# The same hybrid block with its SBUF tile pools placed at other ends of the memory

## The chip, the cores and the metric

The kernel runs on one NeuronCore of a Trainium2 chip. The metric is the device time of one execution in microseconds, lower is better; a time that is given for a kernel is the median of several runs.

## What is computed

One layer of a hybrid decoder trunk on 512 tokens of 1024 features, in float32. Its matrix products are the bulk of it:

```python
h = _rmsnorm(x, g_mix)
proj = h @ w_in                       # 1024 -> 7424: LRU, gelu gate, q, k, v, memory q, 3 branch gates
y_lru = (gelu(gate_lru) * rg_lru(conv(x_lru))) @ w_lru_out
y_dil = dilated_attention(q, k, v, rel_bias) @ w_dil_out
y_mem = cross_attention(q_mem, _rmsnorm(mem, g_mem) @ w_mem_kv) @ w_mem_out
merged = gt[0] * y_lru + gt[1] * y_dil + gt[2] * y_mem
x = x + merged @ w_out
x = x + jnp.square(jax.nn.relu(_rmsnorm(x, g_mlp) @ w_mlp_in)) @ w_mlp_out
y = _rmsnorm(x, g_final)
```

## The kernel before, in words

**Precision and the three products.** Each float32 operand of a large product is split in two float32r parts: a high part (`whi`, `hT_hi`, `ah`, ...) that ScalarE makes by a copy, and a remainder (`wlo`, `hT_lo`, `al`, ...) that VectorE makes by a subtraction. A product is then three matmuls into one PSUM bank: high by high, high by low, low by high. Weights come as a raw slab by DMA from SyncE's queue (`raw`, two buffers), are split by `split_w` (line 162) into `whi` and `wlo` (four buffers each), and are used.

**Two kinds of product.** A matmul has a stationary operand (128 columns, brought in by a weight load, PEld in the profile) and a moving one (here mostly 512 columns).
- `mm3` (lines 186 to 195) makes features by tokens: the *weights* are stationary and the activations move. Per row block k it issues L191 (`whi` with the high activation), L192 (`whi` with the low one), L193 (`wlo` with the high one). The moving tiles are `hT_hi`, `hT_lo` (the normalised, transposed x), later `hmT_hi`, `hmT_lo` (the same for the MLP), and for the branch projections `y`, `odh`/`odl` and `omh`/`oml`.
- `out_step` (lines 932 to 938) makes tokens by features: the *activations* are stationary and the weights move. It issues L936 (high activation, `whi`), L937 (high activation, `wlo`), L938 (low activation, `whi`). It is used for the output projection, where the activations are the eight `mrg` tiles, and for the second MLP product. The trace names the weights before the activations there, as in `ps<-whi,act`.
- `v_proj` (L513 to L515) and the value half of the memory projection (L763 to L765) have the second form too, with `hT` and `mT` as the stationary side. `half_proj` (L247 to L251) has the first with 256 columns.

**The MLP.** It runs in four quarters of 1024 hidden features: `mlp_in(q + 1)` is issued ahead of `mlp_out(q)`. `mlp_evac` (line 973) writes the eight hidden chunks of a quarter: the first three into two tiles each of a ring called `q` (names `ah` and `al`), the other five into one pair tile each, `act`, which holds the high and the low part. `mlp_out` goes twice (two column halves) through k = 0 to 7 and within each k through the four token tiles: 36 matmuls of 512 columns that load `ah` or `al`, then 60 that load `act`. The last half of the last quarter goes token tile by token tile, and its last tile in two pieces of 256 columns.

**Order.** TensorE's order is the program's own, interleaved by a hand-written clock (`_Interleave`): attention and LRU steps are slipped between the dense groups. The other engines' instructions are placed by the tile framework.

**Where tiles lie.** A tile pool takes its place in each partition of SBUF when it is opened. Before, the pools stand one above the other in the order in which they are opened: `cst`, `big`, `wp` (raw and split weights), `sm` (small statistics), and on top of them the pool of the stage: `start`, then `lru`, then `att`, then `ep`. So the weights lie in the middle, `hT` and the rings `q`, `V` and `y4` below them, and the stage's own tiles above.

Of the kernel before, what the change touches and what calls it, by code (L numbers as in the profile page):

```python
# [17 lines left out]
P = 128  # L18
# [34 lines left out]
def _bucket_onehots():  # L53
    """[33, 3, 384]: column m of group g picks the bias row at its offset; row 32 marks masked offsets."""
    oh = np.zeros((NUM_BUCKETS + 1, 3, 384), np.float32)
    m = np.arange(384)
    for g in range(3):
        if g == 0:
            off = 255 - m
            valid = (off >= 0) & (off <= 128)  # L60
            dist = off
        elif g == 1:
            off = 127 - m
            valid = off >= 0
            dist = 4 * off
        else:
            off = 127 - m
            valid = (off >= 0) & (off % 4 == 0)
            dist = 4 * off
        b = _bucket(np.maximum(dist, 0))  # L70
        for j in m:
            oh[b[j] if valid[j] else NUM_BUCKETS, g, j] = 1.0
    return oh


def _head_select():
    """[4, 2, 128]: column p of pair hp picks head 2*hp + p // 64."""
    s = np.zeros((HPG, 2, P), np.float32)
    for hp in range(2):
        for p in range(P):  # L80
            s[2 * hp + p // HD, hp, p] = 1.0
    return s


class _Engine:
    """An engine whose instructions can be pinned to program order."""
# [16 lines left out]
class _Interleave:  # L103
    """Program order: dense matmul groups advance a clock; side generators yield the delay (in us of
    tensor-engine work) that their next step should stay behind."""
# [34 lines left out]
def hybrid_block(ctx: ExitStack, tc: tile.TileContext, x, mem, g_mix, w_in, b_gate, conv_w, conv_b,  # L140
# [7 lines left out]
    cst = ctx.enter_context(tc.tile_pool(name="cst", bufs=1))  # L148
    big = ctx.enter_context(tc.tile_pool(name="big", bufs=1))
    wp = ctx.enter_context(tc.tile_pool(name="wp", bufs=1))  # L150
    sm = ctx.enter_context(tc.tile_pool(name="sm", bufs=1))
# [24 lines left out]
    def slab(parts):  # L176
        """parts: (weight, first column) of 128 columns each; yields the split halves one by one."""
        raw = raw_tile(KT, 256)
        if parts[0][0] is parts[1][0] and parts[0][1] + P == parts[1][1]:
            nc.sync.dma_start(raw, cols(parts[0][0], parts[0][1], 256))  # L180
        else:
            for i, (w, c0) in enumerate(parts):
                nc.sync.dma_start(raw[:, :, i * P:(i + 1) * P], cols(w, c0, P))
        return [split_w(raw[:, :, i * P:(i + 1) * P], KT, P) for i in range(len(parts))]

    def mm3(ps, w, act, nk, k0=0, us=0.648):
        """ps = w.T @ act over nk row blocks, w = (hi, lo) stationary, act(k) -> (hi, lo) moving."""
        whi, wlo = w
        for k in range(nk):
            ah, al = act(k)  # L190
            PE.matmul(ps, whi[:, k0 + k, :], ah, start=k == 0, stop=False)  # L191
            PE.matmul(ps, whi[:, k0 + k, :], al, start=False, stop=False)  # L192
            PE.matmul(ps, wlo[:, k0 + k, :], ah, start=False, stop=k == nk - 1)  # L193
            if k % 2 == 1 and k < nk - 1:
                sch.tick(2 * us)
        # the caller ticks the rest after its evacuation

# [9 lines left out]
    def rstd(xt, sq, tag):  # L207
        """sq: scratch as wide as xt; returns [P, 1] rsqrt(mean(x^2) + eps)."""
        ss = sm.tile([P, 1], F32, name="ss", tag="ss" + tag, bufs=2)
        A.activation(sq, xt, AF.Square, accum_out=ss)  # L210
        return rstd_of(ss, tag)
# [12 lines left out]
    def transp(hn, dst, t):  # L224
        """hn [tokens, D] of token tile t, transposed and split into dst = (hi, lo)."""
        for half in range(2):
            ps = psum()
            for k in range(4):
                c = half * 4 + k
                PE.transpose(ps[:, k * P:(k + 1) * P], hn[:, c * P:(c + 1) * P], ident)  # L230
            pv = ps.rearrange("p (k n) -> p k n", k=4)
            hv = dst[0][:, half * 4:half * 4 + 4, t * P:(t + 1) * P]
            A.activation(hv, pv, AF.Copy)
            V.tensor_sub(dst[1][:, half * 4:half * 4 + 4, t * P:(t + 1) * P], pv, f(hv))
# [4 lines left out]
    def half_proj(items, act, evac, mid):  # L239
        """items: split stationaries; two token halves, the second after mid() was emitted."""  # L240
# [21 lines left out]
    T0 = big.tile([P, HPG, 256], F32, name="T0")  # L262
    T12 = big.tile([P, HPG, 2, P], F32, name="T12")
# [12 lines left out]
    # the tensor engine's clock gate opens while the first tokens are on their way  # L276
# [19 lines left out]
    # per-feature vectors, one column per 128 features  # L296
# [49 lines left out]
    def lru_gate(c, xc, xh, xlo, rg_hi, rg_lo):  # L346
# [12 lines left out]
        # t = tanh(-log(a) / 2) = (1 - a) / (1 + a); 1 / (1 + t) starts from (1 + a) / 2  # L359
# [22 lines left out]
    def start_rest():  # L382
        """the other two token tiles, the constants, then what the first LRU chunk needs."""
        for t in (2, 3):
            transp(hns[t], hT, t)

    def small_consts():
# [9 lines left out]
        # Toeplitz bias tiles: 128 copies of each vector, read back with a row pitch one short  # L397
# [16 lines left out]
    # softplus(-lam) = max(-lam, 0) + log1p(exp(-|lam|)), log1p(e) = 2 atanh(e / (2 + e))  # L414
# [52 lines left out]
    # block-diagonal recurrence gates, two 64-blocks per 128 features  # L467
# [14 lines left out]
    def qk_proj(g, nm):  # L482
        """two chunks (heads 0-1, 2-3) of q (scaled) or k; groups 1, 2 in residue order (t mod 4, t // 4)."""
        o = (O_Q if nm == "q" else O_K) + g * 256
        res = []
        for w in slab([(w_in, o), (w_in, o + P)]):
            ps = psum()
            mm3(ps, w, hmov, KT)
            t_ = q2k(nm)
            sc = 0.125 if nm == "q" else 1.0  # L490
            if g == 0:
                A.activation(t_, ps, AF.Copy, scale=sc)
            else:
                A.activation(t_.rearrange("p (r i) -> p r i", r=4), ps.rearrange("p (i r) -> p r i", r=4),
                             AF.Copy, scale=sc)
            res.append(t_)
            sch.tick(1.3)
        return res

    def v_proj(g):  # L500
        """[128 tokens, 4 token tiles, 256]; token tile = block for group 0, residue for groups 1, 2,
        which are brought to residue order on their way through DRAM."""
        vt = big.tile([P, 4, 256], F32, name="vt", tag="V", bufs=4)
# [18 lines left out]
        vr = big.tile([P, 4, 256], F32, name="vr", tag="V", bufs=4)  # L522
# [3 lines left out]
    def vtile(name):  # L526
        return big.tile([P, D], F32, name=name, tag="V", bufs=4)

    # memory tokens, normalised here and transposed once there is room
# [44 lines left out]
    def softmax_stats(sc, mz, i):  # L574
        """sc [P, 4 heads, n]: exp(s - max) in place; mz[:, 0|1, i, :] = max, sum."""
# [11 lines left out]
    def p_T(groups):  # L587
        """groups of 4 [128, 128] slices, transposed; returns SBUF tiles [128 keys, 4, 128 queries]."""
# [32 lines left out]
    def av_out(dst, view, terms):  # L621
        """terms: (transposed P [keys, 4, queries], V [keys, 256]) summed into [128, 2 head pairs, 128]."""
# [38 lines left out]
    def stats_T(mz, permute):  # L661
        """mz [P tokens, 2, 4 tiles, 4 heads] -> [4 heads, 2, 512 tokens] in token order."""
# [15 lines left out]
    def side_b():  # L678
# [13 lines left out]
        # merge by the softmax denominators  # L692
# [156 lines left out]
    def pair_m():  # L849
        return big.tile([P, 2, S], F32, name="m", tag="V", bufs=4)  # L850

    def pair_gate(c2, b):
        tg = big.tile([P, 2, S], F32, name="tg", tag="V", bufs=4)
# [56 lines left out]
    def act_tile(name):  # L910
        return ep.tile([P, 2, S], F32R, name=name, tag="act", bufs=10)
# [61 lines left out]
    def mlp_evac(act, ps):  # L973
        i = len(act)
        r = big.tile([P, 2, S], F32, name="rl", tag="V", bufs=4)
# [3 lines left out]
        else:  # L979
            t_ = act_tile("act")  # L980
# [96 lines left out]
```

## Time and profile before

| | us |
|---|---|
| median of three runs | 894.89 |
| lowest and highest run | 893.42 and 896.57 |
| span of the profiled execution, first to last instruction | 892.8 |
| TensorE busy in that span | 879.6 |
| VectorE, ScalarE, GpSimd busy | 451.6, 356.7, 26.0 |

The page gives no time of its own for the profiled execution; its span is 2.1 us under the median of the runs. TensorE's busy time is a union of matmuls that overlap in the pipeline: one matmul of 512 columns shows about 390 ns, yet the next one starts some 230 ns later. How fast TensorE goes is therefore read from the starts in the timeline (start to start), not from the durations. A duration still tells fast and slow matmuls apart, because it is longer by as much as the next start is later.

### The profile page before, as it was taken

How to read it: one execution, taken by the hardware profiler on the slowest of the kernel's cores; microseconds unless marked ns; L12 is line 12 of the kernel's file. 1: busy time of each engine (PE TensorE's matmuls, PEld its weight loads, DVE VectorE, ACT ScalarE, POOL GpSimd, SP SyncE). 2: the span in 40 equal slices, each digit the busy share in tenths (PEclk: the TensorE clock that was granted, in tenths of full speed). 3: DMA queues.
4: the chain of work that ended last, by engine and by line, in shares of the span. 5: the costliest groups of instructions: out<-in, count | busy, mean ns of one | idle time of the engine just before them, and what ended most of it. 6: DMA issues, size and time to landing. Idle time of an engine off the chain costs nothing.

```text
span 892.8 us, 10656 instructions
## 1 busy us (share of the span) xinstructions
PE 879.6 (99%) x4383; PEld 734.8 (82%) x4383; DVE 451.6 (51%) x628; ACT 356.7 (40%) x565; POOL 26.0 (3%) x34
## 2 busy tenths in 40 slices
PE   8999999999999999999999999999999999999997
PEld 7788888889888888888888888888888888888886
DVE  5778666764678543343424365444334433443342
ACT  5457666654644532332323154433113311441122
POOL 3110000000000000000000000000000000000020
PEclk9899999999999999999999999999999999999999
DMA  7673333333421222332434214322333323332202
GB/s 239 186 227 95 95 95 95 95 111 127 140 85 60 70 96 71 118 97 81 130 133 160 83 46 144 95 94 96 94 96 97 106 90 97 111 105 93 98 6 94
DMA packets 79164, 94.87 MB, mean 106 GB/s; under 512 B 3611, under 2 KB 64103, under 8 KB 78988
## 3 DMA queue, kind: packets, MB, share of 16 engines
q1 hardware_dynamic: 77916, 88.15, 31.6%
q0 software_dynamic: 1056, 5.52, 1.9%
q8 instruction: 34, 0.56, 0.3%
q10 hardware_dynamic: 144, 0.52, 0.1%
q14 instruction: 14, 0.11, 0.0%
HBM read 91.03 MB, written 5.52 MB: 108 GB/s over the span
## 4 chain that ended last, share of the span: by engine, by line
PE 92%; DVE 2%; DMA 2%; ACT 1%; issue 1%; POOL 0%; SPq 0%; POOLq 0%; ACTq 0%; DVEq 0%
PE ps L191 19%; PE ps L192 19%; PE ps L193 18%; PE ps L938 8%; PE ps L936 8%; PE ps L937 8%; PE ps L513 1%; PE ps L515 1%; PE ps L514 1%; DMA x<-in_x_dram 1%; PE ps L248 1%; PE ps L626 1%; PE ps L247 1%; PE ps L593 1%; PE ps L251 1%
## 5 line engine op out<-in xcount | busy, mean ns | idle before, releaser
L95 DVE TENSOR_TENSOR wlo<-raw,whi 128x1024 fp32r<-128x1024 f32 (+1 forms) x153 | 182.9, 1199 | 314.2 <-ACT whi L95 309.7
L95 ACT ACTIVATE whi<-raw 128x1024 fp32r<-128x1024 f32 (+1 forms) x154 | 159.5, 1037 | 394.2 <-PE ps L192 223.0
L191 PE MATMUL ps<-hT_hi,whi 128*128 128x512 f32 x400 | 156.6, 392 | 0.0
L193 PE MATMUL ps<-hT_hi,wlo 128*128 128x512 f32 x400 | 155.9, 390 | 0.0
L192 PE MATMUL ps<-hT_lo,whi 128*128 128x512 f32 x400 | 155.9, 390 | 0.0
L192 PE MATMUL ps<-hmT_lo,whi 128*128 128x512 f32 x240 | 93.4, 389 | 0.0
L193 PE MATMUL ps<-hmT_hi,wlo 128*128 128x512 f32 x240 | 93.4, 389 | 0.0
L191 PE MATMUL ps<-hmT_hi,whi 128*128 128x512 f32 x240 | 93.2, 389 | 0.0
L191 PEld LDWEIGHTS ps<-hT_hi,whi 128*128 128x128 f32 x400 | 75.1, 188 | 16.4 <-issue 0.6
L193 PEld LDWEIGHTS ps<-hT_hi,wlo 128*128 128x128 f32 x400 | 75.1, 188 | 15.8
L192 PEld LDWEIGHTS ps<-hT_lo,whi 128*128 128x128 f32 x400 | 75.1, 188 | 15.2
L938 PE MATMUL ps<-whi,act 128*128 128x512 f32 (+1 forms) x165 | 64.1, 389 | 0.0
L937 PE MATMUL ps<-wlo,act 128*128 128x512 f32 (+1 forms) x165 | 64.1, 388 | 0.0
L936 PE MATMUL ps<-whi,act 128*128 128x512 f32 (+1 forms) x165 | 64.1, 388 | 0.0
L192 PEld LDWEIGHTS ps<-hmT_lo,whi 128*128 128x128 f32 x240 | 45.1, 188 | 9.3
L191 PEld LDWEIGHTS ps<-hmT_hi,whi 128*128 128x128 f32 x240 | 45.0, 188 | 9.4
L193 PEld LDWEIGHTS ps<-hmT_hi,wlo 128*128 128x128 f32 x240 | 45.1, 188 | 9.3
L95 DVE TENSOR_TENSOR x<-x,ps 128x512 f32<-128x512 f32 (+1 forms) x41 | 27.7, 675 | 24.9 <-PE ps L938 24.6
L938 PE MATMUL ps<-whi,al 128*128 128x512 f32 (+1 forms) x99 | 38.0, 384 | 0.0
L937 PE MATMUL ps<-wlo,ah 128*128 128x512 f32 (+1 forms) x99 | 37.9, 383 | 0.0
L936 PE MATMUL ps<-whi,ah 128*128 128x512 f32 (+1 forms) x99 | 37.9, 383 | 0.0
L937 PEld LDWEIGHTS ps<-wlo,act 128*128 128x128 f32 x165 | 31.0, 188 | 7.1
(253 smaller groups left out, 1355.6 us busy)
## 6 DMA issues: line engine op xcount, KB each, us to landing
raw<-in_w_in_dram SPq DMA_DIRECT2D x23, 1024.0 KB
raw<-in_w_mlp_in_dram SPq DMA_DIRECT2D x16, 1024.0 KB
raw<-in_w_mlp_out_dram SPq DMA_DIRECT2D x16, 1024.0 KB
raw<-in_w_in_dram SPq DMA_DIRECT2D x12, 512.0 KB
raw<-in_w_mem_kv_dram SPq DMA_DIRECT2D x4, 1024.0 KB
raw<-in_w_out_dram SPq DMA_DIRECT2D x4, 1024.0 KB
x<-in_x_dram SPq DMA_DIRECT2D x7, 512.0 KB
raw<-in_w_lru_out_dram SPq DMA_DIRECT2D x4, 768.0 KB
```

The lines of the kernel that those rows point to most:

```text
L95: r = fn(*a, **k)
L191: PE.matmul(ps, whi[:, k0 + k, :], ah, start=k == 0, stop=False)
L192: PE.matmul(ps, whi[:, k0 + k, :], al, start=False, stop=False)
L193: PE.matmul(ps, wlo[:, k0 + k, :], ah, start=False, stop=k == nk - 1)
L247: PE.matmul(ps[:, sl], whi[:, k, :], ah, start=k == 0, stop=False)
L248: PE.matmul(ps[:, sl], whi[:, k, :], al, start=False, stop=False)
L251: PE.matmul(ps[:, sl], wlo[:, k, :], act[0][:, k, sl], start=False, stop=k == KT - 1)
L513: PE.matmul(ps[:, 0:256], ah, hi[:, k % 4, :], start=k == 0, stop=False)
L514: PE.matmul(ps[:, 0:256], ah, lo[:, k % 4, :], start=False, stop=False)
L936: PE.matmul(ps, ah[:, sl], hi[:, k % 2, :], start=k == 0, stop=False)
L937: PE.matmul(ps, ah[:, sl], lo[:, k % 2, :], start=False, stop=False)
L938: PE.matmul(ps, al[:, sl], hi[:, k % 2, :], start=False, stop=k == KT - 1)
```

## The change

Four edits, and comments and docstrings taken out (later lines stand three further down in the new kernel):

- `sm` and `wp` are opened with `side="right"`: they are allocated from the high end of SBUF downwards.
- A new pool `ot`, also from the high end, takes tiles that only VectorE, ScalarE and DMAs use, or that `v_proj` makes: `T0`, `T12` and the ring `V`, which were in `big`.
- The pair tiles `act` have a ring of eight instead of ten, and the fourth hidden chunk of each quarter goes into a ring of `big` (`y4`, six buffers, of which the residual tiles `x2` hold four), under the name `act3`.
- All else stays in `cst`, `big` and the stage pools, which are now allocated from the low end without the weights between them.

```diff
     cst = ctx.enter_context(tc.tile_pool(name="cst", bufs=1))
     big = ctx.enter_context(tc.tile_pool(name="big", bufs=1))
-    wp = ctx.enter_context(tc.tile_pool(name="wp", bufs=1))
-    sm = ctx.enter_context(tc.tile_pool(name="sm", bufs=1))
+    sm = ctx.enter_context(tc.tile_pool(name="sm", bufs=1, side="right"))
+    wp = ctx.enter_context(tc.tile_pool(name="wp", bufs=1, side="right"))
+    ot = ctx.enter_context(tc.tile_pool(name="ot", bufs=1, side="right"))
...
-    T0 = big.tile([P, HPG, 256], F32, name="T0")
-    T12 = big.tile([P, HPG, 2, P], F32, name="T12")
+    T0 = ot.tile([P, HPG, 256], F32, name="T0")
+    T12 = ot.tile([P, HPG, 2, P], F32, name="T12")
...
-        vt = big.tile([P, 4, 256], F32, name="vt", tag="V", bufs=4)
+        vt = ot.tile([P, 4, 256], F32, name="vt", tag="V", bufs=4)
...
-        return ep.tile([P, 2, S], F32R, name=name, tag="act", bufs=10)
+        return ep.tile([P, 2, S], F32R, name=name, tag="act", bufs=8)
...
-        r = big.tile([P, 2, S], F32, name="rl", tag="V", bufs=4)
+        r = ot.tile([P, 2, S], F32, name="rl", tag="V", bufs=4)
...
-            t_ = act_tile("act")
+            t_ = act_tile("act") if i > 3 else big.tile([P, 2, S], F32R, name="act3", tag="y4", bufs=6)
```

(The other tiles of the ring `V`, which are `vr`, `mn`, `msq`, `gbmem`, `m` and `tg`, go from `big` to `ot` in the same way.)

The built programs hold the same instructions in the same order on every engine. One wait is added: the DMA that loads `gbmlp` (SyncE's queue, line 237) also waits for the first software DMA, `bd<-bvec`. What changes is the addresses. In KiB from the start of a partition, as the two programs have them:

| tiles | used by TensorE as | before | after |
|---|---|---|---|
| `ident` | moving (transposes) | 16 | 16 |
| `hT_hi`, `hT_lo`, `hmT_hi`, `hmT_lo` | moving, in `v_proj` stationary | 18.3 to 50.3 | 18.3 to 50.3 |
| ring `q` (`q`, `k`, `ah`, `al`, `omh`, `odh`, ...) | moving or stationary | 74.3 to 98.3 | 50.3 to 74.3 |
| ring `y4` (`y`; after, `act3` too) | moving; `act3` stationary | 98.3 to 122.3 | 74.3 to 98.3 |
| `whi`, `wlo` | stationary in `mm3`, moving in `out_step` | 138.3 to 170.3 | 190.4 to 222.4 |
| `mT`, later `qmh`, `qml` | moving or stationary | 171.8 to 187.8 | 98.3 to 114.3 |
| `mrg`, `act` (ring of 10, then of 8) | stationary | 171.8 to 211.8 | 98.3 to 130.3 |
| `xh`, `xlo` / `rg_hi`, `rg_lo` | moving / stationary | 181.9 to 189.9 / 197.9 to 209.9 | 108.3 to 116.3 / 124.3 to 136.3 |
| `pr`, `prm` | stationary (transposes) | 187.8 to 199.8 | 114.3 to 126.3 |
| `pT`, `pTh`, `pTl` | moving | 199.8 to 207.8 | 126.3 to 134.3 |
| `km` / `vm` | moving / stationary | 207.8 to 215.8 / 215.8 to 223.8 | 134.3 to 142.3 / 142.3 to 150.3 |
| `vt`, `vr`, `mn` (ring `V`) | stationary | 58.3 to 74.3 | 158.4 to 174.4 |
| `raw` | not used | 122.3 to 138.3 | 174.4 to 190.4 |

## Rows read from the trace of the kernel before

**Rows 1.** The page: busy time by engine, TensorE's clock, the chain that ended last.
```profile
PE 879.6 (99%) x4383; PEld 734.8 (82%) x4383; DVE 451.6 (51%) x628; ACT 356.7 (40%) x565; POOL 26.0 (3%) x34
...
PEclk9899999999999999999999999999999999999999
...
PE 92%; DVE 2%; DMA 2%; ACT 1%; issue 1%; POOL 0%; SPq 0%; POOLq 0%; ACTq 0%; DVEq 0%
```

**Rows 2.** Matmuls grouped by line and shape: count | busy us, mean ns | idle.
```profile
L193 PE MATMUL ps<-hT_hi,wlo 128*128 128x512 f32 x400 | 155.9, 390 | 0.0
...
L192 PE MATMUL ps<-hmT_lo,whi 128*128 128x512 f32 x240 | 93.4, 389 | 0.0
...
L938 PE MATMUL ps<-whi,act 128*128 128x512 f32 x155 | 61.3, 396 | 0.0
...
L936 PE MATMUL ps<-whi,ah 128*128 128x512 f32 x93 | 36.2, 389 | 0.0
...
L938 PE MATMUL ps<-whi,mrg 128*128 128x512 f32 x64 | 25.3, 395 | 0.0
...
L192 PE MATMUL ps<-y,whi 128*128 128x512 f32 x48 | 18.7, 389 | 0.0
```

**Rows 3.** Timeline, TensorE, second MLP product: from `al` to `act`. Start us, duration us.
```profile
629.43 0.40 PE L938 MATMUL ps<-whi,al 128*128 128x512 f32 x1
629.67 0.39 PE L936 MATMUL ps<-whi,act 128*128 128x512 f32 x1
```

**Rows 4.** Timeline, TensorE: the last `act` of that half, then `ah` again.
```profile
643.43 0.40 PE L938 MATMUL ps<-whi,act 128*128 128x512 f32 x1
643.66 0.39 PE L936 MATMUL ps<-whi,ah 128*128 128x512 f32 x1
```

**Rows 5.** Timeline, TensorE: the first `act` of the next column half.
```profile
651.83 0.39 PE L936 MATMUL ps<-whi,act 128*128 128x512 f32 x1
```

**Rows 6.** Timeline, TensorE: the last `mm3` matmul before the output projection.
```profile
484.74 0.40 PE L193 MATMUL ps<-omh,wlo 128*128 128x512 f32 x1
```

**Rows 7.** Matmuls grouped by line and shape: smaller groups with both operands above 138 KiB.
```profile
L191 PE MATMUL ps<-mT_hi,whi 128*128 128x256 f32 x32 | 9.4, 295 | 0.0
...
L764 PE MATMUL ps<-wlo,mT_hi 128*128 128x512 f32 x16 | 6.3, 395 | 0.0
...
L351 PE MATMUL ps<-xlo,rg_hi 128*128 128x512 f32 x12 | 4.7, 395 | 0.0
...
L797 PE MATMUL ps<-km,qmh 128*128 128x256 f32 x16 | 4.5, 281 | 0.0
```

**Rows 8.** Timeline, TensorE, 256 columns, `qmh` by `km`: first of twelve, and what follows.
```profile
275.48 0.28 PE L796 MATMUL ps<-km,qmh 128*128 128x256 f32 x1
...
276.90 0.39 PE L191 MATMUL ps<-hT_hi,whi 128*128 128x512 f32 x1
```

**Rows 9.** Timeline, TensorE, 256 columns, `v_proj`: first, and the 28th.
```profile
80.87 0.28 PE L513 MATMUL ps<-whi,hT_hi 128*128 128x256 f32 x1
...
84.11 0.28 PE L513 MATMUL ps<-whi,hT_hi 128*128 128x256 f32 x1
```

**Rows 10.** Matmuls grouped by line and shape: transposes and the attention's value product.
```profile
L593 PE MATMUL ps<-ident,pr 128*128 128x128 f32 x60 | 8.6, 274 | 0.2 <-ACT pr L95 0.2
...
L626 PE MATMUL ps<-pT,vr 128*64 128x128 f32 x64 | 4.6, 282 | 0.0
...
L626 PE MATMUL ps<-pT,vt 128*64 128x128 f32 x56 | 4.1, 282 | 1.0 <-ACT pT L95 1.0
...
L230 PE MATMUL ps<-ident,mn 128*128 128x128 f32 x16 | 2.1, 272 | 0.0
```

**Rows 11.** ScalarE's largest group by line and shape, same columns.
```profile
L95 ACT ACTIVATE whi<-raw 128x1024 fp32r<-128x1024 f32 x146 | 154.4, 1059 | 367.4 <-PE ps L192 196.2 <-PE ps L938 107.6 <-DVE x L95 27.2
```

**Rows 12.** GpSimd's queue early on, and the view of the tile `gbmlp`.
```profile
38.70 0.56 POOL L95 DMA_DIRECT2D bw<-bd  x1 [2.66 <-DMA bd<-bvec]
...
L237 SPq DMA_DIRECT2D gbmlp<-in_g_mlp_dram x1: 341/341/341, 320.6 to 320.6; - x1
```

More of the change, by code (lines that the diff above doesn't have):

```diff
@@ L521, in v_proj @@
         G.dma_start(vd.rearrange("(t p) d -> p t d", p=P), vt)
-        vr = big.tile([P, 4, 256], F32, name="vr", tag="V", bufs=4)
+        vr = ot.tile([P, 4, 256], F32, name="vr", tag="V", bufs=4)
         G.dma_start(vr, vd.rearrange("(i r) d -> i r d", r=4))
@@ L526, in vtile @@
     def vtile(name):
-        return big.tile([P, D], F32, name=name, tag="V", bufs=4)
+        return ot.tile([P, D], F32, name=name, tag="V", bufs=4)
     mr = mem.rearrange("o (t p) d -> p (o t) d", p=P)
@@ L849, in pair_m @@
     def pair_m():
-        return big.tile([P, 2, S], F32, name="m", tag="V", bufs=4)
+        return ot.tile([P, 2, S], F32, name="m", tag="V", bufs=4)
     def pair_gate(c2, b):
-        tg = big.tile([P, 2, S], F32, name="tg", tag="V", bufs=4)
+        tg = ot.tile([P, 2, S], F32, name="tg", tag="V", bufs=4)
         for e, w in enumerate(slab([(w_in, O_G + b * D + c2 * 256), (w_in, O_G + b * D + c2 * 256 + P)])):
```

## The prediction, made before the changed kernel ran

> **What bounds the kernel now.** I read the page first. TensorE is busy in 879.6 of 892.8 us, the chain that ends last is 92% TensorE, and its clock is granted in full after the first slices [rows 1]. So time is saved only if TensorE's stream of matmuls gets shorter. The change touches no instruction of that stream; it moves operands to other addresses. The question is whether the trace shows a matmul's pace to depend on where its operands lie. For that I read the matmuls grouped by line and shape, and then, since durations overlap, the starts in the timeline.
>
> The groups already differ. All the 512-column matmuls that stream an activation from the low tiles past a weight from the middle take 389 or 390 ns, as do those of the second MLP product that load `ah`. Those that load `act` or `mrg`, with the same weights streaming, take 395 or 396 [rows 2]. The timeline turns that into pace. From the first `act` at 629.67 [rows 3] to the first `ah` at 643.66 [rows 4] lie 60 matmuls: 13.99 us / 60 = 233.2 ns each. From there to the next `act` at 651.83 [rows 5] lie 36: 8.17 / 36 = 226.9 ns. Same line numbers, same weights, same shapes, no wait between; only the address of the loaded activation differs (below 98.3 KiB against above 171.8). The excess is **6.3 ns a matmul**. It sets in with the last matmul of `al`, which takes 0.40 us (the `ah` group averages 0.389 [rows 2]): while it runs, the first `act` is being loaded for the next one [rows 3]. So the excess comes from a stream and a load that run at the same time.
>
> Which addresses collide? Slow: streams at 138 to 170 KiB with loads at 172 to 212 (`act`, `mrg`) [rows 2], the same with `mT`, and streams at 182 to 190 with loads at 198 to 210 (`rg`) [rows 7]. Fast: streams at 18 to 122 KiB (`hT`, `hmT`, `y`) with loads at 138 to 170, and the reverse, streams at 138 to 170 with loads at 74 to 98 (`ah`) [rows 2]. Distance does not sort them: `y` lies as little as 16 KiB under the weights and is fast, `act` up to 70 KiB above them and slow. An edge between 122.3 KiB (the end of the highest `y`) and 138.3 (the first `whi`) sorts all of it: slow when stream and load lie on the same side. 128 KiB is in that gap.
>
> **The change, part by part.**
>
> *`act` and `mrg` to 98.3 to 130.3 KiB, weights to 190.4 to 222.4.* The trace has 155 matmuls of 512 columns on each of three lines for `act` and 64 on each of three for `mrg` [rows 2]: 3 x 219 = 657. All are on the path. 657 x 6.3 ns = **4.14 us off**. Not all the way: of the ring's eight slots the topmost runs from 126.3 to 130.3, so that its low part begins above 128 KiB; it is one of three loads in one of eight slots, 657 / 24 = 27 matmuls, 0.17 us that stay. If the edge is right above 122.3 KiB instead, two of eight slots stay slow and the gain is three quarters, 3.1 us. The fourth hidden chunk (`act3`) goes to 78 to 86 KiB, clearly low. That ring has two slots left beside `x2`, and its reuse lies two quarters back, as that of `act` does: no new wait.
>
> *`mm3`.* Streams stay at 18 to 98 KiB or so, loads go from 138 to 170 up to 190 to 222. They were on opposite sides and still are: 0. This is the term that could turn the sign; it is priced with the rivals.
>
> *Smaller groups that come apart.* Three lines of 16 matmuls for the memory values (`mT`) and three of 12 for the gates (`rg`) have 512 columns and take 395 ns against 389 [rows 2, 7]. The first 48 come apart wholly, 48 x 6 ns = 0.29 us; of the gates only part, since `rg_lo` lies above 130 KiB. I take 0.35 us off for both; the bounds are 0.2 and 0.5.
>
> *256 columns.* Here the rows speak the other way. Twelve matmuls of `qmh` by `km`, all above 171 KiB, take 276.90 - 275.48 = 1.42 us, 118.3 ns each [rows 8]; 27 of `v_proj`, low loads under middle streams, take 84.11 - 80.87 = 3.24 us, 120.0 ns each [rows 9]. 144 such matmuls come apart (three lines of 32 for `mT`, three of 16 for `qmh` by `km` [rows 7]): 144 x 1.7 = **0.24 us on**.
>
> *Transposes and the value product.* `ident` streams at 16 KiB; `mn` (58 to 74, same side) takes 272 ns, `pr` (above 187, other side) 274 [rows 10]. Placement shows nothing at 128 columns. The 120 value products [rows 10] go from opposite sides to mostly the same one. No row has them so: bounds are 0, by the transposes of the same width, and 120 x 6.3 = 0.76 us, by the 512-column excess. I take 0, the nearer shape.
>
> *What feeds TensorE.* ScalarE stands idle 367 us before its weight splits, some 300 of it until TensorE is done with a buffer [rows 11]. So the splits wait for TensorE and not the other way round, and 4 us less of matmuls is covered: no new wait, 0.
>
> *The added wait.* `gbmlp` is issued at 320.6 us, and the software DMA that it now waits for had landed by 38.7 [rows 12]: 0. Behind it in SyncE's queue stand the weight loads, which would be late if it were not.
>
> **Sum:** -4.14 + 0.17 - 0.35 + 0.24 = -4.1 us. The bounds of its terms give from -2.7 (edge at 122: -3.1 - 0.2 + 0.24, and half of the 0.76 on) to -4.4 (nothing stays in the ring, 0.5 off for the small groups). The span goes from 892.8 to 888.7. The runs' median lies 2.1 us above the profiled span, so 894.9 - 4.1 = **890.8 us**.
>
> The Trainium skill (TensorE: Matmul & The Clock Gate, "What happens when you issue a matmul") says the opposite of what I rest on: TensorE has two independent SBUF read ports, so loading the next weights does not take read bandwidth from the running matmul. SBUF — State Buffer, "Who interferes with whom", agrees that TensorE waits for nobody. By that rule placement is worth nothing and the sum is 0, a time of 894.9; its chance is part of that of the no-change rival below. The trace disagrees, with 233.2 against 226.9 ns for the same line and the same weights [rows 3 to 5].
>
> **The rivals.**
>
> *Slower: the high load, not the shared side.* Perhaps a weight load from the top of SBUF is slow whatever streams. For it: at 484.74 a `wlo` matmul that streams `omh` (92 KiB, low) is already at 0.40 us while the first `mrg` (171.8) is loaded [rows 6]; by sides it should be fast. Against it: at the end of an `act` run the matmul at 643.43 is still at 0.40 us although the load beside it is `ah` [rows 4], so single matmuls at the edge of a run are blurred and prove little; and `wlo` reaches 170.3 KiB with fast loads in 400 matmuls [rows 2], so that the limit would have to fall in the 1.5 KiB up to the first `mrg`. If it is so, the 512-column `mm3` matmuls of `hT`, `hmT` and `y` alone, 3 x (400 + 240 + 48) = 2064 [rows 2], get the excess: 13.0 us on, against 4.1 off, 894.9 + 8.9 = 903.8 us. It decides the sign once a load at 190 to 222 KiB costs more than 4.1 us / 2064 = 2.0 ns.
>
> *No change.* The excess may go with something other than the address that `act` and `mrg` share: both are pair tiles of two 512-column parts, `ah` and `al` single ones. For it: the pair layout survives the change. Against it: the access pattern of one load is the same 128 adjacent columns, and `y`, also a pair tile, is fast as a stream [rows 2]. A place late in k is not it: `mrg` is there from k = 0 to 7, and all its matmuls average 395 [rows 2]. Time: 894.9, or 895.1 with the 256-column term.
>
> **How the numbers follow.** Forecast 0.80, slower rival 0.08, no change 0.12. The likeliest case's own range is its bounds, -2.7 to -4.4 us, widened by how far single runs lie from their median (1.7 us): 888.8 to 893.9. The range for 8 in 10 reaches from there up to the no-change case, 888.8 to 895.0, and leaves out the slower one. A measurement of this kernel can tell about 0.3%, 2.7 us, from no change. The forecast passes that, but by only 1.4 us, which is less than the runs scatter: 0.66 of its 0.80 count as faster and 0.14 as the same. With the no-change case mostly in "same": faster 0.67, same 0.25, slower 0.08.
>
> **What would show it.** In the profile of the changed kernel the `act` and `mrg` groups should stand at 389 to 390 ns, the 60 matmuls of an `act` run should take 13.6 us instead of 14.0, and the `hT` and `hmT` groups should stay at 389 or 390. `hT` groups at 395 mean the slower rival; `act` at 395 means no change. `mT` by weights with 256 columns should go from 118 to 120 ns. I am wrong in size if the top slot of the ring stays slow beyond its low part (an edge lower than 128), and wrong in kind if TensorE shows new idle time.

## The result, and the profile after

The changed kernel takes **909.27 us** (median of five runs, 908.76 to 909.59) against 894.89: ratio 1.0161, 95% interval 1.0149 to 1.0173. It is slower by 14.4 us, where 4.1 us faster were forecast. Its profiled execution took 908.84 us with a span of 906.8, which is 14.0 us more than the span before.

The page of the changed kernel: busy time by engine, the granted clock, the chain that ended last.

```profile
span 906.8 us, 10656 instructions
...
PE 893.1 (98%) x4383; PEld 733.0 (81%) x4383; DVE 451.8 (50%) x628; ACT 356.4 (39%) x565; POOL 24.9 (3%) x34
...
PEclk9999999999999999999999999999999999999999
...
PE 92%; DVE 2%; DMA 2%; ACT 1%; issue 1%; POOL 0%; SPq 0%; POOLq 0%; ACTq 0%; DVEq 0%
```

Against [rows 1], TensorE's busy time grew by 13.5 us with the same number of matmuls. VectorE and ScalarE are where they were, the mean granted clock is 0.996 of full speed (0.995 before), so the upper of its two levels, 2.4 GHz, in both, and the chain is 92% TensorE as before. So no wait was added on that chain; TensorE's own stream became slower. The groups by line and shape of the changed kernel say where (count, busy us, mean ns, idle):

```profile
L196 PE MATMUL ps<-hT_hi,wlo 128*128 128x512 f32 x400 | 157.3, 393 | 0.0
...
L195 PE MATMUL ps<-hmT_lo,whi 128*128 128x512 f32 x240 | 95.7, 399 | 0.0
...
L941 PE MATMUL ps<-whi,act 128*128 128x512 f32 x155 | 61.4, 396 | 0.0
...
L939 PE MATMUL ps<-whi,ah 128*128 128x512 f32 x93 | 36.9, 397 | 0.0
...
L941 PE MATMUL ps<-whi,mrg 128*128 128x512 f32 x64 | 25.4, 396 | 0.0
...
L195 PE MATMUL ps<-y,whi 128*128 128x512 f32 x48 | 19.1, 399 | 0.0
```

These answer to [rows 2], three line numbers further down. `act` and `mrg`, which should have come down from 396 and 395, stayed. `hT`, `hmT`, `ah` and `y`, which should have stayed at 389 or 390, went up to 393 to 399. The timeline gives the pace in the second MLP product (first `act`, first `ah`, next `act`):

```profile
638.88 0.39 PE L939 MATMUL ps<-whi,act 128*128 128x512 f32 x1
...
652.94 0.40 PE L939 MATMUL ps<-whi,ah 128*128 128x512 f32 x1
...
661.38 0.40 PE L939 MATMUL ps<-whi,act 128*128 128x512 f32 x1
```

60 matmuls of `act` take 14.06 us, 234.3 ns each (before: 233.2, [rows 3, 4]). The 36 of `ah` and `al` take 8.44 us, 234.4 each (before: 226.9, [rows 4, 5]). There is no fast and slow kind left: of all distances between 512-column matmuls 98% are above 229.5 ns (before: 27%), though streams and loads now lie on opposite sides.

The bill, from the distances between starts in both traces, summed by group:

| group | us more |
|---|---|
| 512 columns: `hT`, `hmT`, `y` (2064 matmuls) | +13.0 |
| 512 columns: `ah`, `al` (279) | +2.0 |
| 512 columns: `omh`, `oml`, `odh`, `odl`, and the smaller groups | +0.9 |
| 512 columns: `act`, `mrg` (657) | +0.7 |
| 256 columns, the gaps behind them included | -1.8 |
| narrower ones, the gaps behind them included | -0.8 |
| sum, the span's growth | +14.0 |

### The profile page after: what moved, and what is told of

Its sections match the earlier page's. It is cut to its first block, busy times and chain, and to the rows that moved or that the text cites. A ratio compares the mean times of both kernels' runs of the same rounds, so it can differ in the third digit from the quotient of the medians.

```text
span 906.8 us, 10656 instructions
## 1 busy us (share of the span) xinstructions
PE 893.1 (98%) x4383; PEld 733.0 (81%) x4383; DVE 451.8 (50%) x628; ACT 356.4 (39%) x565; POOL 24.9 (3%) x34
## 4 chain that ended last, share of the span: by engine, by line
PE 92%; DVE 2%; DMA 2%; ACT 1%; issue 1%; POOL 0%; SPq 0%; POOLq 0%; ACTq 0%; DVEq 0%
PE ps L195 19%; PE ps L194 19%; PE ps L196 19%; PE ps L939 8%; PE ps L941 8%; PE ps L940 8%; PE ps L516 1%; PE ps L518 1%; PE ps L517 1%; DMA x<-in_x_dram 1%; PE ps L629 1%; PE ps L251 1%; PE ps L250 1%; PE ps L596 1%; PE ps L254 1%
## 5 line engine op out<-in xcount | busy, mean ns | idle before, releaser
L194 PE MATMUL ps<-hT_hi,whi 128*128 128x512 f32 x400 | 159.3, 398 | 0.0
L195 PE MATMUL ps<-hT_lo,whi 128*128 128x512 f32 x400 | 158.5, 396 | 0.0
L196 PE MATMUL ps<-hT_hi,wlo 128*128 128x512 f32 x400 | 157.3, 393 | 0.0
L195 PE MATMUL ps<-hmT_lo,whi 128*128 128x512 f32 x240 | 95.7, 399 | 0.0
L196 PE MATMUL ps<-hmT_hi,wlo 128*128 128x512 f32 x240 | 94.1, 392 | 0.0
L196 PEld LDWEIGHTS ps<-hT_hi,wlo 128*128 128x128 f32 x400 | 75.1, 188 | 18.6
L195 PEld LDWEIGHTS ps<-hT_lo,whi 128*128 128x128 f32 x400 | 75.1, 188 | 16.9
L196 PEld LDWEIGHTS ps<-hmT_hi,wlo 128*128 128x128 f32 x240 | 45.1, 188 | 10.7
L195 PEld LDWEIGHTS ps<-hmT_lo,whi 128*128 128x128 f32 x240 | 45.1, 188 | 10.4
L941 PEld LDWEIGHTS ps<-whi,act 128*128 128x128 f32 x165 | 31.1, 188 | 7.1
```

The source lines that it names most:

```text
L941: PE.matmul(ps, al[:, sl], hi[:, k % 2, :], start=False, stop=k == KT - 1)
```

## The experiments

The edge in the forecast had fallen with this trace. What was left to explain: what do `hT`, `y` and `ah` before share with the weights that `act` before, and everything after, does not? The two programs also differ in something that the table of KiB ahead of the prediction rounds away: the remainder of the start addresses. `sm` holds a few dozen tiles of 4 to 128 bytes, each rounded up to 32, so whatever lies beyond it starts at an odd place. Before, that is the stage's tiles, `act` and `mrg` among them; after, it is the weights. All 512-column operands repeat in steps that are multiples of 512 bytes (a row of one k, a buffer of a ring), so that a tile keeps one remainder modulo 256 all through. The table gives it for the first kernels that ran, in bytes as their built programs have them, with the mean distance between the starts of the 3260 matmuls of 512 columns (distances over 260 ns left out), and the time. The ratio is to the kernel before as it ran beside each of them (medians of 894.7 to 895.0 us):

| kernel | `hT`, `y`, `ah` | `act`, `mrg` | weights | ns | us | ratio to before |
|---|---|---|---|---|---|---|
| before | 32 | 64 | 32 | 228.4 | 894.89 | |
| after | 32 | 32 | 192 | 233.6 | 909.27 | 1.0161 |
| after, weights down 32 | 32 | 32 | 160 | 232.3 | 905.74 | 1.0120 |
| before, `act` up 32 | 32 | 96 | 32 | 228.4 | 893.46 | 0.9987 |
| after, low side up 32 | 64 | 64 | 192 | 232.3 | 907.35 | 1.0140 |
| before, all up 32 | 64 | 96 | 64 | 228.4 | 894.56 | 1.0000 |
| after, weights down 160 | 32 | 32 | 32 | 226.9 | **889.53** | 0.9949 |
| before, `act` down 32 | 32 | 32 | 32 | 226.9 | **889.19** | 0.9939 |
| before, weights up 128 | 32 | 192 | 160 | 232.9 | 907.55 | 1.0151 |
| before, weights up 256 | 32 | 192 | 32 | 228.6 | 895.93 | 1.0016 |

**First four: the top of SBUF, or the alignment?** Each kernel gets one tile of 32 bytes that nothing uses, so that what lies behind it moves by 32.

```diff
+    sm.tile([P, 8], F32, name="pad")       # e1 in the changed kernel, e2 in the one before
...
+    cst.tile([P, 8], F32, name="pad")      # e3 in the changed kernel, e4 in the one before
```

Weights of the changed kernel 32 bytes down:

> The changed kernel with one unused tile of 32 bytes in the pool sm: the weights and the ring V lie 32 bytes lower (whi at 194976 instead of 195008 bytes, 32 instead of 0 above a multiple of 64), still in the top of SBUF; hT, act and the rest stay (32 above a multiple of 64). Theory A (a stream and a load whose starts differ by 32 bytes modulo 64 slow each other, wherever they lie): all 512-column matmuls at 389 ns, about 227 ns start to start, 890 us. Theory B (an operand above some 171 KiB is slow, whatever its offset): nothing changes, 909 us. Theory C (an operand at a multiple of 64 bytes is slow): 890 us as A.

Tiles above the weights of the kernel before, 32 bytes up:

> The kernel before with one unused tile of 32 bytes in the pool sm: the stage pools on top (act, mrg, mT, rg) lie 32 bytes higher (act at 175968 instead of 175936 bytes, now 32 above a multiple of 64, as the weights are); weights and all below stay. Stream and load of the second MLP product are on the same side of SBUF as before. Theory A: act and mrg go from 395 to 389 ns, 4 us off, 890.8 us. Theory B (top addresses slow) and the prediction's own view (same side slow): nothing changes, 894.9. Theory C: 890.8.

All but weights and `ot` of the changed kernel, 32 bytes up:

> The changed kernel with one unused tile of 32 bytes in the pool cst: everything on the low side lies 32 bytes higher (hT_hi at 18752, act at 100672 bytes: multiples of 64), the weights stay at a multiple of 64. Theory A (only the difference modulo 64 counts): all 512-column matmuls at 389 ns, 890 us. Theory B (top slow): 909. Theory C (multiples of 64 slow): 909 or more.

Everything of the kernel before, 32 bytes up:

> The kernel before with one unused tile of 32 bytes in the pool cst: everything lies 32 bytes higher, so hT and the weights are now at multiples of 64 and act, mrg, mT and rg are 32 above one; all differences stay. Theory A: nothing changes, 894.9 us, act at 395 and hT at 390 ns. Theory B: 894.9. Theory C: hT by weights slow, 395 ns, and act by weights slow too, 908 us or more.

Measured: 905.74 (903.47 to 907.91), 893.46 (891.98 to 895.73), 907.35 (907.11 to 907.51) and 894.56 us (893.10 to 895.54). The same remainder modulo 64 is not enough (theory A): in the first three kernels the slow streams and loads share it, and stay slow. The first row is `hT` in the first kernel, the second `act` in the second:

```profile
L197 PE MATMUL ps<-hT_hi,wlo 128*128 128x512 f32 x400 | 157.8, 394 | 0.0
```

```profile
L937 PE MATMUL ps<-whi,act 128*128 128x512 f32 x155 | 61.3, 396 | 0.0
```

But in the first and the third something moved: 232.3 ns instead of 233.6, with 84% of the distances above 229.5 ns instead of 98%. An address that matters only through its side, or its height (theory B), can't do that by 32 bytes. The fourth moved all operands by 32 bytes together, onto and off multiples of 64, and nothing changed: theory C falls, and no address tried so far mattered by itself. That left the difference between stream and load, modulo something larger than 64: 0 was the only fast one so far; 32, 64, 128 and 160 were slow.

**The next four: the same remainder on opposite sides, and on one.**

```diff
+    sm.tile([P, 40], F32, name="pad")                            # e5, in the changed kernel
...
-        ng, ab, ee, zz, z2, acc = (tiny(n) for n in ("ng", "ab", "ee", "zz", "z2", "acc"))
+        ng, ee, zz, z2, acc = (tiny(n) for n in ("ng", "ee", "zz", "z2", "acc"))
-        V.tensor_tensor(ab, ng, lam, op=ALU.max)
-        A.activation(ee, ab, AF.Exp, scale=-1.0)
+        V.tensor_tensor(ee, ng, lam, op=ALU.max)                 # e6, in the kernel before: one
+        A.activation(ee, ee, AF.Exp, scale=-1.0)                 # 32-byte tile less in sm
...
+    gp = ctx.enter_context(tc.tile_pool(name="gp", bufs=1))      # e7, before wp; in e8 64 floats,
+    gp.tile([P, 32], F32, name="pad")                            # and tags of sm shared for room
```

> The changed kernel with an unused tile of 160 bytes in the pool sm: the weights start at 194848 bytes, so that weights, hT, the ring q, y4, act and mrg all have the same remainder modulo 512 bytes (288), as hT, q, y4 and the weights had in the kernel before. They are on opposite sides, the weights in the top. Theory D (stream and load must have the same remainder modulo 256 or 512 bytes to be fast; in all slow pairs seen so far they have not): all 512-column matmuls at 389 ns, 890 us. Theory B (an operand above some 171 KiB is slow): 905 to 909 us, 395 ns.

> The kernel before with one tiny tile of 32 bytes saved in the pool sm (the softplus works in place): the stage pools on top lie 32 bytes lower, act and mrg at 175904 bytes and up, the same remainder modulo 512 as the weights (288). Stream and load of the second MLP product stay on one side of SBUF, above 138 KiB. Theory D: act and mrg go from 395 to 389 ns, 4 us off, 890.8 us. Theory B, and the prediction's own view (same side slow): 894.9 us, 395 ns.

> The kernel before with an unused pool of 128 bytes opened between big and wp: the weights and all above them lie 128 bytes higher, at 138.4 KiB instead of 138.3, so that hT, q and y4 differ from them by 128 modulo 512. Theory D: nearly every 512-column matmul at 394 ns or more, 905 to 909 us. Theory B: nothing changes, 894.9.

> The kernel before with a gap of 256 bytes between big and wp (the room comes from statistics tiles in sm that share their tags): weights 256 modulo 512 above hT, q and y4. If theory D holds with 256 bytes: hT by weights stays at 389 ns, 894.9 us; with 512 bytes: slow, 905 to 909. Theory B: 894.9.

Measured: **889.53** (888.68 to 890.26), **889.19** (887.48 to 890.47), 907.55 (907.14 to 907.96) and 895.93 us (894.37 to 898.83). These settle it. The first keeps every pool where the change put it, weights on top, all operands on opposite sides, and only slides the weights down by 160 bytes: 909.3 becomes 889.5. Its rows, in the order of those of after:

```profile
L197 PE MATMUL ps<-hT_hi,wlo 128*128 128x512 f32 x400 | 155.7, 389 | 0.0
...
L196 PE MATMUL ps<-hmT_lo,whi 128*128 128x512 f32 x240 | 93.4, 389 | 0.0
...
L942 PE MATMUL ps<-whi,act 128*128 128x512 f32 x155 | 60.3, 389 | 0.0
...
L940 PE MATMUL ps<-whi,ah 128*128 128x512 f32 x93 | 36.2, 389 | 0.0
```

The second leaves every pool on its side. `act` and `mrg` lie above the weights, as in the kernel before, on what the prediction called the same side. They come down 32 bytes, and the excess is gone; the first `act` and the first `ah` of its timeline:

```profile
628.46 0.39 PE L936 MATMUL ps<-whi,act 128*128 128x512 f32 x1
...
642.06 0.39 PE L936 MATMUL ps<-whi,ah 128*128 128x512 f32 x1
```

60 matmuls in 13.60 us, 226.7 ns each, against 233.2 in the same place before [rows 3, 4]. Over the whole trace the 657 matmuls of `act` and `mrg` take 4.3 us less. The third takes the kernel before out of step, as the change did: weights moved by half of 256, sides kept, and the groups that had been fast are slow.

```profile
L195 PE MATMUL ps<-hT_hi,wlo 128*128 128x512 f32 x400 | 157.9, 395 | 0.0
...
L194 PE MATMUL ps<-hmT_lo,whi 128*128 128x512 f32 x240 | 94.7, 394 | 0.0
```

In the fourth they are 256 bytes up and `hT` and `hmT` by the weights are fast again (392 and 389 in the first two rows; the line of `hT_hi` by `whi` has a mean of 392 in the kernel before too), while `act`, now 160 from the weights, stays slow:

```profile
L193 PE MATMUL ps<-hT_hi,whi 128*128 128x512 f32 x400 | 156.8, 392 | 0.0
...
L194 PE MATMUL ps<-hmT_lo,whi 128*128 128x512 f32 x240 | 93.4, 389 | 0.0
...
L939 PE MATMUL ps<-wlo,act 128*128 128x512 f32 x155 | 61.8, 399 | 0.0
```

So what counts repeats every 256 bytes, not every 128 (three kernels of the table are 128 apart and slow) and not only every 512.

**How small a difference, and is there more to gain?** The kernel with 32 bytes saved (889.19), with the LRU's `xl` padded from 515 to 576 floats, so that `xh` and `rg` share the weights' remainder too; and the kernel before with `hT` read 16 bytes and `hmT` 4 bytes further up in tiles that are 256 bytes larger (tags of `sm` shared for room, by which `act` and `mrg` also come to lie 160 from the weights instead of 32; they stay slow).

```diff
-        xl = lpool["p"].tile([P, S + 3], F32, name="xl", bufs=2)
+        xl = lpool["p"].tile([P, 576], F32, name="xl", bufs=2)[:, 0:S + 3]     # e9
...
+    def shifted(name, tag, o):                                                 # e10
+        return big.tile([P, KT * S + 64], F32R, name=name, tag=tag)[:, o:o + KT * S].rearrange("p (k s) -> p k s", k=KT)
+    hT = (shifted("hT_hi", "hT_hi", 4), shifted("hT_lo", "hT_lo", 4))
...
+            hmT = (shifted("hmT_hi", "hT_hi", 1), shifted("hmT_lo", "hT_lo", 1))
```

> The kernel before with 32 bytes saved in sm, as in the run that moved the top pools down by 32, and the LRU's xl tile padded from 2060 to 2304 bytes, so that xh, xlo, rg_hi and rg_lo too have the remainder of the weights modulo 256. Theory D: act and mrg at 389 ns as there, and the gate matmuls (rg) go from 395 to 390; 0.2 to 0.4 us less than that run, 889.0 us. If the gates' slowness comes from the switch between groups instead: 889.2, rg at 395.

> The kernel before with hT and hmT in tiles that are 256 bytes longer, of which a view is used that starts 16 bytes in (hT) and 4 bytes in (hmT); the weights keep the remainder of the tiles' start modulo 256. Theory D taken strictly (any difference modulo 256 is slow): hT by weights 394 ns, hmT by weights 394 ns, 907 us. Theory D with a grain of 32 bytes (only the line of 32 bytes counts, differences inside it are free): both at 389 ns, 895 us. With a grain between 4 and 16: hT slow, hmT fast, 902 us.

Measured: 889.96 us (888.22 to 890.31), no better than 889.19, since there are only 36 such matmuls; and 906.89 (906.56 to 907.21). The 36 tell something all the same. Without the padding `xh` and `rg` agree with each other (both 96 modulo 256) and yet two of their three lines are slow; with it, agreeing with their neighbours too, they are fast. First without, then with:

```profile
L352 PE MATMUL ps<-xh,rg_lo 128*128 128x512 f32 x12 | 4.7, 396 | 0.0
...
L350 PE MATMUL ps<-xh,rg_hi 128*128 128x512 f32 x12 | 4.7, 393 | 0.0
L351 PE MATMUL ps<-xlo,rg_hi 128*128 128x512 f32 x12 | 4.7, 388 | 0.0
```

```profile
L350 PE MATMUL ps<-xh,rg_hi 128*128 128x512 f32 x12 | 4.7, 389 | 0.0
L351 PE MATMUL ps<-xlo,rg_hi 128*128 128x512 f32 x12 | 4.7, 389 | 0.0
L352 PE MATMUL ps<-xh,rg_lo 128*128 128x512 f32 x12 | 4.7, 389 | 0.0
```

And neither 16 nor 4 bytes are free: 4 cost as much as any other difference, or more. In the kernel with 16 and 4 bytes (the first row is `hT`, the second `hmT`, the third `y`, which was not shifted):

```profile
L193 PE MATMUL ps<-hT_hi,wlo 128*128 128x512 f32 x400 | 157.6, 394 | 0.0
L193 PE MATMUL ps<-hmT_hi,wlo 128*128 128x512 f32 x240 | 96.2, 401 | 0.0
...
L193 PE MATMUL ps<-y,wlo 128*128 128x512 f32 x48 | 18.7, 390 | 0.0
```

From start to start that is 231.6 ns for `hT` and 238.2 for `hmT` on this line, against 227.6 and 226.5 in the kernel before. One thing stays open here: these streams also start off a multiple of 32 bytes, which none of the other kernels' do, and no run moves stream and load off it together. So whether 4 and 16 bytes cost through the difference, as the larger shifts do, or through the odd start itself, is not shown.

**Which pair has to agree?** The kernel before with 128 bytes between the `whi` buffers and the `wlo` buffers; and the kernel before with `act` and `mrg` in step with the weights, only the low parts of `hT` and `hmT` read 128 bytes further up (tags of `sm` shared again).

```diff
+        if not padded:                                               # e12, ahead of the first wlo
+            padded.append(wp.tile([P, 32], F32, name="pad"))
...
-           big.tile([P, KT, S], F32R, name="hT_lo", tag="hT_lo"))
+           shifted("hT_lo", "hT_lo", 32))                            # e13, hmT_lo alike; a pad of 96
                                                                      # bytes in sm evens out the rest
```

> The kernel before with an unused tile of 128 bytes between whi and wlo in the pool wp: wlo, and all above, lie 128 bytes higher; whi keeps the remainder of hT, hmT, q and y4. Theory D1 (the stream collides with the load that runs beside it, the next one's): of the three lines of mm3 L192's matmul (low activation streams, wlo is being loaded) is the slow one; one third of the excess or less, about 899 us. Theory D2 (a matmul's own two operands must agree): the wlo line is the slow one. If one slow load in three is enough to spoil all three: 907 us.

> As in the kernel with 32 B saved, all weights, act, mrg, y and the high parts of hT and hmT start at the same remainder modulo 256 (32); only the low parts hT_lo and hmT_lo are read 128 B further up. Nothing is left out of the computation. The loads are all alike; of three matmuls of one k only the middle one (L196, which streams the low part) differs from its loads. Theory 'a matmul is slow where its stream's remainder differs from its own load's or from the next load's': of the groups of hT and hmT only the middle one is slow (about 233 ns from start to start, 640 matmuls x 6.5 ns = 4.2 us), its neighbours stay at 227; time 889.2 + 4.2 = 893.4 us. Theory 'one odd matmul also spoils the one behind it': two of three slow, about 897.5 us. Theory 'what counts is that successive loads have the same remainder, whatever streams': all fast, 889.2 us. Theory 'any disturbance spoils the whole stretch': all three slow, about 901.6 us.

Measured: 904.26 us (902.82 to 905.70), and 894.64 (893.53 to 899.70). One load in three out of step spoils two matmuls of three, always the same two; from the timeline of the first kernel:

```profile
450.45 0.39 PE L195 MATMUL ps<-hT_hi,whi 128*128 128x512 f32 x1
450.68 0.40 PE L196 MATMUL ps<-hT_lo,whi 128*128 128x512 f32 x1
450.91 0.40 PE L197 MATMUL ps<-hT_hi,wlo 128*128 128x512 f32 x1
```

Over all 400 of each line, from start to start: 227.0 for L195, 232.4 for L196 (beside it `wlo` is loaded for the next) and 234.0 for L197 (it streams past that `wlo`). In the second MLP product of the same kernel, where `ah` and `al` are loaded, only the line that streams `wlo` is slow (234.1, its neighbours 226.7 and 226.9):

```profile
L941 PE MATMUL ps<-wlo,ah 128*128 128x512 f32 x93 | 36.7, 395 | 0.0
L940 PE MATMUL ps<-whi,ah 128*128 128x512 f32 x93 | 36.2, 389 | 0.0
L942 PE MATMUL ps<-whi,al 128*128 128x512 f32 x93 | 36.2, 389 | 0.0
```

(Where `act` is loaded all three lines are slow, 231.9 to 234.7: it lies above `wlo` and moved up with it, so that it is 160 bytes from `whi` and 32 from `wlo`.) All this fits one rule: a matmul is slow where its stream disagrees with its own load or with the load of the next one. The last kernel was made to test that rule, and gives it half. Of its three lines the middle one, which streams the low part (L193 in the built kernel), is slow (over 229.5 ns) in 74% of the `hT` matmuls and 78% of the `hmT` ones. But its neighbours, whose loads and streams agree, are slow too in 25 to 56% of theirs. The rows of `hmT`, where a line without slow matmuls shows 389:

```profile
L193 PE MATMUL ps<-hmT_lo,whi 128*128 128x512 f32 x240 | 94.5, 394 | 0.0
L194 PE MATMUL ps<-hmT_hi,wlo 128*128 128x512 f32 x240 | 93.8, 391 | 0.0
L192 PE MATMUL ps<-hmT_hi,whi 128*128 128x512 f32 x240 | 93.7, 391 | 0.0
```

The time of the kernel does not decide between the rule's 893.4 us and the 897.5 of two slow ones in three: the median lies near the first, the profiled execution, at 897.47, on the second, and the ten runs spread over 6 us. The gates break the rule outright. They come as six matmuls in a row that agree among themselves, so that only the last has a differing load beside it; yet the first six of the kernel before start 236, 233, 236, 224, 231 and 231 ns apart. So a disagreement also lingers, and the rule is good for the long runs only.

## Why the prediction was wrong

**Right: what bounds the kernel, and that only the pace of TensorE's stream could move it.** TensorE's busy time grew by 13.5 of the 14.0 us, and the distances between 512-column matmuls alone by 16.6. The added wait on `gbmlp` cost nothing: the DMA is issued at 322.3 us instead of 320.6 [rows 12], and the profile shows nothing that waited for its tile. ScalarE's idle time before its splits grew, from 367.4 [rows 11] to 383.0 us, as it would behind a slower TensorE.

**Right: the excess itself.** 6.3 ns a matmul, from a stream and a load that run together, was nearly right: 6.5 separate 226.7 from 233.2 ns for the same 60 matmuls, with and without 32 bytes. In the kernel with `wlo` alone moved, L196 agrees with its own load and differs only from the next one, and takes 232.4 ns. The statement of the Trainium skill that loading the next tile's weights takes no read bandwidth from the running matmul (TensorE: Matmul & The Clock Gate, "What happens when you issue a matmul"), which the prediction weighed, is at odds with that number.

**Wrong: the step "An edge between 122.3 and 138.3 KiB sorts all of it".** It sorted the groups that I had, and so does the remainder modulo 256, which I had not looked at: the table gave addresses in KiB to one decimal, and 32 bytes are 0.03 KiB. Before, `hT`, `hmT`, `y`, `q` and the weights all start at 32 modulo 256, and `mT`, `act` and `mrg` at 64, only because `sm` lies between the two sets. In all the large groups side and remainder went together. That was a confounded observation, and I gave it 0.80. Only the gates could have warned: `xh` and `rg` share the remainder (128) and still show 395 on one line [rows 7], which the edge explains and the rule above does not.

**Wrong by consequence: "*`mm3`* ... 0".** This term carried the error: +13.0 us for 2064 matmuls, the very number worked out for the slower rival. `ah` and `al` add 2.0 us which no case had, because both the edge and the rival left them fast. And the 4.1 us off for `act` and `mrg` did not come, since their difference to the weights only went from 32 to 160. Nor did the 0.35 us off for the smaller groups: the `mT` and `rg` lines of 512 columns together changed by less than 0.1 us.

**The slower rival** had the right sign, the right term and, with 903.8 us, missed by 5.5, at a chance of 0.08. That its 13.0 us came out was luck, because its mechanism was wrong as well: a load from the top of SBUF is not slow. In the kernel with weights 160 bytes down they lie between 190.3 and 222.3 KiB, and the `hT`, `hmT` and `y` lines take 226.3 to 227.3 ns.

**Dismissed too early: the matmuls at the edge of a run.** The 0.40 us of `wlo` by `omh` while the first `mrg` is loaded [rows 6] and of the last `act` while `ah` is loaded [rows 4] I called blurred. By the rule above neither is: the first streams past the load of its successor, which is 32 bytes off, the second past its own load, which is too. Two rows that the edge could not both explain should have cost it more than they did.

**Not seen: 256 columns.** Before, `v_proj` has equal remainders and takes 120.0 ns a matmul [rows 9]; after, with unequal ones, it takes 117.7. The sign is reversed there, and `v_proj` gave back 0.7 of the 1.8 us in the table above. This, not sides, may be the difference between [rows 8] and [rows 9]: `qmh` and `km` agree with each other but not with the weights around them, and in the kernel with 32 bytes saved, where they agree with these too and lie only 32 bytes lower, the median of each of their lines is 120.0 instead of 118.5 or 119.0. No run was made for this alone. The 0.24 us on that the prediction gave its 144 matmuls of 256 columns came out near, at 0.17, but it went by the wrong property.

**What the gain really was.** The 4.1 us were there to be had (4.3 on `act` and `mrg`), by 32 bytes in `sm` and with every pool on its side: 889.19 us, ratio to the kernel before 0.9939 (0.9921 to 0.9957). The change with its weights slid into step has the same, 0.9949 (0.9934 to 0.9964). Since both are alike, opposite halves are worth nothing that these runs can tell.

## What to carry to other kernels

Where a stream of matmuls like these (512 columns of float32r, a weight load for each) is the bound, look at the byte addresses of both operands modulo 256 in the built program before anything else about their place, and look again after every edit that adds, drops or resizes even a tile of a few bytes in a pool below them. Here one 32-byte tile was worth 0.6%, and a shift of half a period cost 1.5%. And where two properties of an address sort the rows equally well, give neither the forecast alone: write down every property that the rows share before choosing one.

## What was not expected of the hardware

- A 512-column float32r matmul with a weight load beside it has the next one start 226 to 229 ns later, by the mean of a line, where in a long run both operands' addresses agree modulo 256 bytes, and 231 to 239 ns later where they do not. Differences of 32, 64, 128 and 160 bytes were all slow, 0 and 256 fast, whatever the side of SBUF; 4 and 16 were slow too, with starts off a multiple of 32.
- The slow pace is not one number. With 160 bytes the three lines of `hmT` stand at 232.0, 237.0 and 231.1 ns, in a fixed pattern; with 128 bytes, 16% of the distances are under 229.5 in the first and third kernel above, and nearly half on two lines of `hT` in the kernel before with weights up 128; with 4 bytes, all three lines stand at 237 to 239.
- A disagreement lingers: matmuls that agree in all their own operands are partly slow behind ones that do not. How long, and what in the reading of the two operands causes it, these runs leave open. So is whether other types or widths have the same period.
